# Gate's and the first units' products of a third's first block ahead of the second block's tiles, in the input projection of a hybrid trunk layer

## The chip, the cores and the metric

The kernel runs on one core of one Trainium2 chip. The core has five engines with a queue each: TensorE (PE; its weight loads are shown apart as PEld), VectorE (DVE), ScalarE (ACT), GpSimd (POOL) and SyncE (SP), which here issues nearly all DMA transfers. An engine works through its queue in order, and semaphores tie the engines together. The metric is the device time of one execution in microseconds (us), as a median over runs.

## The reference

One layer of a trunk with three parallel head groups (DEPTH is 1), on 2048 tokens with 16 meta tokens ahead, 1024 wide, all in float32:

```
h = concatenate([meta, x])                          # 2064 tokens x 1024
p = rms_norm(h, norm_mix_pre) @ w_in                # one combined input projection
oa = rg_lru_group(p's first 512 columns)            # gated linear recurrence
ob = forgetting_attention_group(q, k, v, f_logit)   # softmax attention, 8 heads, decay from f_logit
oc = rwkv7_group(the remaining columns)             # matrix-state recurrence over the tokens
h = h + rms_norm(concatenate([oa, ob, oc]) @ w_out, norm_mix_post)
f = causal_dwconv(rms_norm(h, norm_ffn_pre) @ ffn_up)
h = h + rms_norm((gelu(gate) * val) @ ffn_down, norm_ffn_post)
return h[16:]
```

The change concerns the second line alone: the norm of the tokens, and their products with `w_in`. `f_logit` are 8 of its columns (2048 to 2055); the kernel calls their product gate.

## The kernel before

**Stages.** First the input projection (until about 850 us of the profile), with the two recurrences running beside it, then attention with the rest of the recurrences, the output projection, and the feed-forward layer.

**Precision.** A float32 product is made of three: each operand is split into a high part, rounded for TensorE's fast format, and a low part, the remainder, and `mm3` (lines 185 to 189) adds high x high, high x low and low x high in PSUM. So a weight of the projection is a pair `wh`, `wl`, and the tokens are a pair `xh`, `xl`.

**Thirds, blocks, tiles.** The tokens are taken in three thirds (`part` 0, 1, 2), so that the recurrences can begin on a third while the next is projected. `w_in_tokens` cuts 17 tiles (the meta tokens, and 16 of 128) into two blocks for each third: 400 and 384 tokens, 384 and 384, 256 and 256. A tile is brought in by `norm_transpose` (line 133): a load of 128 x 1024 into the ring `nt_x` of four buffers (line 137, SP), the sum of squares (line 124, ACT), the root (lines 127 and 128, DVE and POOL), the scaling (line 142, DVE), eight transposes (line 155, PE), and for each half of the tile the copy `xh` (line 161, ACT) and the remainder `xl` (line 162, DVE). ACT's sum of squares is kept behind the last rounding of weights (`core.rounded`) for the tiles of the second third beyond its first two.

**Gate and units.** `w_in_part` is a generator that runs over a third. `w_in_gate` loads gate's weights `fw` (made in the first third, kept in DRAM, loaded again at line 318), and its `products` takes 16 products on a block (lines 323 and 324), whose two parts ACT and DVE add (lines 326 and 328). Then come 24 units of 128 columns: 8 for RWKV-7, 4 for the RG-LRU, 4 each for k, v and q. A unit's pair of weights is loaded by `w_in_weights` (in the later thirds two transfers of 512 KB from DRAM, line 250), and `w_in_step` makes 24 products on a block (lines 187 to 189), copies the result out of PSUM and stores it. The pairs live in a ring of two (`w`); in the last third every other two units use the ring `nt_x` instead. Before, gate's weights in the later thirds also take one buffer of the ring of pairs, the `wh` side.

**The first third is done otherwise.** Its second block's tiles are held back in `core.unturned`, gate and the first two units are run on the first block, with `core.turn_tile` bringing in one tile after each step, and only then gate and those two units on the second block. In the later thirds, all tiles of both blocks come first, then gate on both blocks, and then the units, each on both blocks. The last two units of every third, both of q, are run together block by block.

**The passages.** A passage is the end of one third and the start of the next. The main loop (lines 2247 to 2304) calls `w_in_norm` for the next third behind the last unit of a third. At each `yield` of `w_in_part` the loop moves the recurrences on by 1.25 steps on average (`Beside`), and at whole units in the later thirds it also issues a step of `w_out_split` and of `up_sums`, whose loads (line 1786, POOL operations at 1788 and 1790) are kept behind the last weight load on SP (`core.loaded`). The recurrences' work on PE near the passages has lines 1159, 1190, 1213, 1218, 1450; on DVE 1171 to 1188 and 1443.

**What sets the order.** The text gives priorities, not the final order. The program is built with

```python
    with _tile.TileContext(nc, schedule_with_timeline_sim=True) as tc:
```

so a planner orders each engine's queue by a modelled time: among the instructions that it takes to be ready, the one earlier in the text goes first. `issue_after` adds an order by hand. The queue is then fixed, and on the chip an instruction that isn't ready holds up all behind it.

Of the kernel before, what the change touches and what calls it, by code (L numbers as in the profile page):

```python
# [194 lines left out]
def w_in_tokens(part):  # L195

    tiles = [(0, META)] + [(META + P * i, P) for i in range(SEQ // P)]
    cuts = ((0, 4, 7), (7, 10, 13), (13, 15, 17))[part]
    return [tiles[a:e] for a, e in zip(cuts, cuts[1:])]


def w_in_norm(core, pools, psum, x, meta, gain, part):
    blocks = []
    for b, tl in enumerate(w_in_tokens(part)):
        t0 = tl[0][0]
        n = sum(r for _, r in tl)
        hi = pools["xn"].tile([P, KD, n], F32R, tag=f"xh{b}", name=core.n("xh"))
        lo = pools["xn"].tile([P, KD, n], F32R, tag=f"xl{b}", name=core.n("xl"))
        blocks.append((t0, n, tl, hi, lo))

    def tile(block, s, rows):
        t0, _, _, hi, lo = block
        src = meta if s < META else x[s - META : s - META + rows, :]
        late = part == 1 and (s, rows) not in blocks[0][2][:2]
        after = (lambda: core.tc.issue_after(core.rounded.ins)) if late else nullcontext
        norm_transpose(core, pools, psum, src, rows, gain, [(hi, lo, s - t0, 0, rows)], after)

    core.unturned = []
    for block in blocks:
        for s, rows in block[2]:  # L220
            if part == 0 and block is blocks[1]:
                core.unturned.append((block, s, rows))
            else:
                tile(block, s, rows)
    core.turn_tile = lambda: tile(*core.unturned.pop(0))
    return blocks


def w_in_kept(scr, c0):

    return scr["wk"][c0 // P]


def w_in_weights(core, pools, w_in, c0, scr, part, raw=None):

    src = w_in[:, c0 : c0 + P].rearrange("(k p) c -> p k c", p=P)
    if raw is not None:
        pair = hi, lo = [pools["w"].tile([P, KD, P], F32R, tag=s, name=core.n(s)) for s in ("wh", "wl")]
        core.loaded = core.nc.sync.dma_start(raw, src)
        core.rounded = core.nc.scalar.activation(hi[:], raw, AF.Copy)  # L240
        core.nc.vector.tensor_tensor(lo[:], raw, hi[:], op=ALU.subtract)
    elif part == 0:
        pair = split_load(core, pools["w"], (pools["nt"], "nt_x", None), src, [P, KD, P], "w")
    else:
        core.turns += part == 2
        pl, tags = (pools["nt"], ("nt_x", "nt_x")) if core.turns % 4 > 1 else (pools["w"], ("wh", "wl"))
        pair = [pl.tile([P, KD, P], F32R, tag=tag, name=core.n(s)) for s, tag in zip(("wh", "wl"), tags)]
    for t, kept in zip(pair, w_in_kept(scr, c0)):
        t = t[:].rearrange("p k c -> p (k c)").bitcast(F32)
        core.loaded = core.nc.sync.dma_start(*((kept, t) if part == 0 else (t, kept)))  # L250
    return pair
# [51 lines left out]
def w_in_gate(core, pools, psum, w_in, blocks, scr, part):  # L303

    nc = core.nc
    c0 = 2048
    home, tag = ("w", "wh") if part else ("us", "us")
    w = pools[home].tile([P, KD, P], F32R, tag=tag, name=core.n("fw"))
    flat, kept = w[:].rearrange("p k c -> p (k c)").bitcast(F32), w_in_kept(scr, 3 * D)[0]
    if part == 0:  # L310
        raw = pools["st"].tile([P, KD, 8], F32, tag="stv", name=core.n("fraw"))
        nc.sync.dma_start(raw[:], w_in[:, c0 : c0 + 8].rearrange("(k p) c -> p k c", p=P))
        nc.vector.memset(w[:].bitcast(F32), 0.0)
        nc.scalar.activation(w[:, :, 0:8], raw[:], AF.Copy)
        nc.vector.tensor_tensor(w[:, :, 32:40], raw[:], w[:, :, 0:8], op=ALU.subtract)
        nc.sync.dma_start(kept, flat)
    else:
        nc.sync.dma_start(flat, kept)

    def products(t0, n, tl, hi, lo):  # L320
        ps = psum.tile([P, 512], F32, tag="mm", name=core.n("psf"))
        for k in range(KD):
            nc.tensor.matmul(ps[:, :n], w[:, k], hi[:, k], start=k == 0, stop=False)
            nc.tensor.matmul(ps[:, :n], w[:, k], lo[:, k], start=False, stop=k == KD - 1)
        a = pools["st"].tile([8, 400], F32, tag="sth", name=core.n("fa"))
        nc.scalar.activation(a[:, :n], ps[32:40, :n], AF.Copy)
        o = pools["st"].tile([8, 400], F32, tag="stl", name=core.n("fo"))
        nc.vector.tensor_tensor(o[:, :n], ps[0:8, :n], a[:, :n], op=ALU.add)
        nc.sync.dma_start(scr["f"][:, t0 : t0 + n], o[:, :n])

    return products


def w_in_part(core, pools, psum, w_in, blocks, scr, part):
    gate = w_in_gate(core, pools, psum, w_in, blocks, scr, part)
    units = [("c", 2056 + P * i) for i in range(8)] + [("a", P * i) for i in range(4)]
    units += [(s, c + P * i) for s, c in (("k", 1024), ("v", 1536), ("q", 512)) for i in range(4)]
    waiting = [None]

    def step(*args):  # L340

        after = w_in_step(core, pools, psum, *args, scr)
        if waiting[0]:
            waiting[0]()
        waiting[0] = after

    if part == 0:
        raws = pools["rp"].tile([P, 2, KD, P], F32, tag="rw_e", name=core.n("raw"))
        firsts = [
            (w_in_weights(core, pools, w_in, c0, scr, part, raws[:, i]), kind, c0)  # L350
            for i, (kind, c0) in enumerate(units[:2])
        ]
        for i, block in enumerate(blocks):
            gate(*block)
            yield i > 0
            for w, kind, c0 in firsts:
                step(w, block, kind, c0)
                if i == 0:
                    core.turn_tile()
                yield i > 0  # L360
            while core.unturned:
                core.turn_tile()
        del units[:2]
    else:
        for block in blocks:
            gate(*block)
        yield False
        yield True

    for kind, c0 in units[:-2]:  # L370
        w = w_in_weights(core, pools, w_in, c0, scr, part)
        for block in blocks:
            step(w, block, kind, c0)
            yield block is blocks[-1]

    last = [(w_in_weights(core, pools, w_in, c0, scr, part), kind, c0) for kind, c0 in units[-2:]]
    for block in blocks:
        for w, kind, c0 in last:
            step(w, block, kind, c0)
            yield kind == "q" and c0 == last[-1][2]  # L380
# [2123 lines left out]
```

## Time and profile before

| | |
|---|---|
| median of 3 runs | 2953.49 us (2950.68 to 2956.22) |
| the profiled execution | 2962.62 us |
| its span, first to last instruction | 2960.9 us |
| mean granted TensorE clock | 0.976 |
| instructions | 53225 |

All rows of the trace are from the one profiled execution; their times count from the start of its span. A row of the timeline has start, length, engine, line, operation, `out<-in` by the program's names, shapes and count, and in brackets the idle time ahead with what ended it. Matmuls overlap, so the length of one (0.34 us) is longer than the distance from one start to the next. The input projection's thirds end near 267 and 597 us.

### The profile page before, as it was taken

The numbers are of one execution on the slowest core, as the hardware profiler recorded it, in microseconds if no ns is written. First come the engines' busy times: TensorE is split into PE (matmuls) and PEld (weight loads), VectorE is DVE, ScalarE is ACT, GpSimd is POOL, SyncE is SP. The second block draws the span as 40 slices with busy tenths as digits, with TensorE's granted clock in tenths as the row PEclk, the third lists the DMA queues.
The fourth block names the chain that finished last, engine by engine and source line by source line (L and its number), as shares of the span: only waits on it lengthen the run. The fifth ranks groups of instructions, "written<-read, shape, count | busy, mean of one in ns | idle before, by whom it ended". The sixth has DMA issues, their size and how long they took to land.

```text
span 2960.9 us, 53225 instructions
## 1 busy us (share of the span) xinstructions
PE 2844.5 (96%) x18854; PEld 2448.4 (83%) x18854; DVE 2002.2 (68%) x3839; ACT 1505.8 (51%) x2937; POOL 1297.3 (44%) x1572
## 2 busy tenths in 40 slices
PE   7998999999978889999999999999999999999998
PEld 7997989989865555566578999999999999787887
DVE  4257654666578765556656998888777787646766
ACT  4236442554346655555635666666566665324333
POOL 1002221222114667666723667355655544656443
PEclk9999999999988999999999999999999999999999
DMA  6776678577653357435255665577777774436453
GB/s 218 248 245 203 198 249 290 166 245 234 203 126 73 87 127 222 108 102 139 58 158 173 209 188 174 164 234 207 215 202 224 218 197 141 146 116 218 149 171 121
DMA packets 470343, 530.51 MB, mean 179 GB/s; under 512 B 86862, under 2 KB 356888, under 8 KB 468524
## 3 DMA queue, kind: packets, MB, share of 16 engines
q1 hardware_dynamic: 469308, 526.18, 58.9%
q8 instruction: 148, 2.42, 0.3%
q0 software_dynamic: 768, 0.93, 0.1%
q14 instruction: 119, 0.97, 0.1%
HBM read 368.07 MB, written 158.90 MB: 178 GB/s over the span
## 4 chain that ended last, share of the span: by engine, by line
PE 69%; DVE 7%; ACT 6%; DMA 5%; issue 2%; POOL 2%; SPq 1%; DVEq 0%; ACTq 0%; POOLq 0%
PE psu L187 9%; PE psu L188 9%; PE psu L189 9%; PE po L779 4%; PE psd L187 4%; PE psd L188 4%; PE psd L189 4%; PE psp L187 2%; PE psp L189 2%; PE psp L188 2%; PE sc L756 2%; PE mx L627 2%; PE sc L757 2%; PE pswo L187 2%; PE pswo L188 2%
## 5 line engine op out<-in xcount | busy, mean ns | idle before, releaser
L188 PE MATMUL psu<-xo,uw 128*128 128x344 f32 x1848 | 591.5, 320 | 0.0
L187 PE MATMUL psu<-xo,uw 128*128 128x344 f32 x1848 | 585.8, 322 | 3.3 <-ACT u L1933 2.3
L189 PE MATMUL psu<-xo,uw 128*128 128x344 f32 x1848 | 582.0, 320 | 0.3 <-DVE uw L1762 0.2
L187 PE MATMUL psp<-xh,wh 128*128 128x384 f32 (+2 forms) x1152 | 383.0, 333 | 0.4 <-DVE rww L1462 0.3
L188 PE MATMUL psp<-xl,wh 128*128 128x384 f32 (+2 forms) x1152 | 378.3, 328 | 0.0
L189 PE MATMUL psp<-xh,wl 128*128 128x384 f32 (+2 forms) x1152 | 375.6, 326 | 0.0
L1762 DVE TENSOR_TENSOR uw<-uq,uw 128x512 fp32r<-128x512 f32 x341 | 319.0, 940 | 60.6 <-ACT uw L1761 57.5
L187 PEld LDWEIGHTS psu<-xo,uw 128*128 128x128 f32 x1848 | 345.8, 188 | 4.8 <-ACT u L1933 2.6
L188 PEld LDWEIGHTS psu<-xo,uw 128*128 128x128 f32 x1848 | 347.1, 188 | 0.0
L189 PEld LDWEIGHTS psu<-xo,uw 128*128 128x128 f32 x1848 | 345.7, 188 | 1.2 <-DVE uw L1762 1.1
L1761 ACT ACTIVATE uw<-uq 128x512 fp32r<-128x512 f32 x462 | 288.1, 627 | 98.1 <-PE psu L189 41.1
L761 ACT ACTIVATE p<-sc,bias 128x512 f32<-128x512 f32 (+4 forms) x352 | 196.8, 590 | 164.3 <-PE sc L757 134.9
L632 DVE TENSOR_REDUCE mc<-mx 128x1 f32<-128x512 f32 (+5 forms) x352 | 191.8, 565 | 113.6 <-PE mx L627 83.7
L1901 DVE SCALAR_TENSOR_TENSOR uy<-psu,ffn_cols,uy 128x342 f32<-128x342 f32 (+1 forms) x390 | 220.5, 567 | 61.1 <-ACT uy L1899 59.7
L1909 POOL TENSOR_TENSOR uy<-uy,uy 128x342 f32<-128x342 f32 (+1 forms) x132 | 145.8, 1105 | 230.6 <-DVE uy L1901 58.4
L1762 POOL TENSOR_TENSOR uw<-uq,uw 128x512 fp32r<-128x512 f32 x121 | 183.3, 1515 | 133.7 <-ACT uw L1761 111.5
L187 PEld LDWEIGHTS psp<-xh,wh 128*128 128x128 f32 x1152 | 220.4, 191 | 7.7 <-issue 4.4
L188 PEld LDWEIGHTS psp<-xl,wh 128*128 128x128 f32 x1152 | 220.5, 191 | 5.6 <-issue 3.9
L189 PEld LDWEIGHTS psp<-xh,wl 128*128 128x128 f32 x1152 | 220.3, 191 | 4.3 <-issue 3.0
L800 POOL TENSOR_TENSOR acc<-acc,p 128x512 f32<-128x512 f32 (+3 forms) x186 | 196.4, 1059 | 49.8 <-DVE acc L800 22.2
L1762 DVE TENSOR_TENSOR fo<-u,fo 128x896 fp32r<-128x896 f32 x88 | 102.0, 1159 | 130.0 <-ACT fo L1761 129.4
L1761 ACT ACTIVATE fo<-u 128x896 fp32r<-128x896 f32 x88 | 81.2, 923 | 205.9 <-PE psd L189 118.3
(492 smaller groups left out, 6289.8 us busy)
## 6 DMA issues: line engine op xcount, KB each, us to landing
uq<-scr_us SPq DMA_DIRECT2D x220, 256.0 KB
uq<-in_ffn_up_dram SPq DMA_DIRECT2D x209, 256.0 KB
wl<-scr_wk SPq DMA_DIRECT2D x48, 512.0 KB
wh<-scr_wk SPq DMA_DIRECT2D x48, 512.0 KB
u<-scr_ff SPq DMA_DIRECT2D x88, 256.0 KB
scr_ff<-uy SPq DMA_DIRECT2D x110, 171.0 KB
raw<-in_w_in_dram SPq DMA_DIRECT2D x24, 512.0 KB
scr_wk<-wh SPq DMA_DIRECT2D x24, 512.0 KB
```

Of the source, the lines that this page charges most:

```text
L187: nc.tensor.matmul(out, ah, bh, start=first, stop=False, skip_group_check=more)
L188: nc.tensor.matmul(out, ah, bl, start=False, stop=False, skip_group_check=more)
L189: nc.tensor.matmul(out, al, bh, start=False, stop=last, skip_group_check=more)
L627: nc.tensor.matmul(ps[:rows, : e - a], q3[:, qo : qo + rows], k2[:, a:e], start=True, stop=not last)
L632: self.reduced = nc.vector.tensor_reduce(mc[:rows, i, ci : ci + 1], ps[:rows, : e - a], axis=AX.X, op=ALU.max)
L761: last = nc.scalar.activation(p[:rows, :w], ps[:rows, :w], AF.Exp, bias=bias[:rows, j : j + 1])
L779: mm = nc.tensor.matmul(po[at : at + 64, c0:n], v1[:rows, j], p[:rows, : n - c0], start=start and i < 2, stop=end and i + 2 >= len(group), ...
L800: eng.tensor_tensor(a, ps_[0][0][:rows, c0:n] if start and i == 1 else a, p[:rows, : n - c0], op=ALU.add)
L1761: core.nc.scalar.activation(hi, src, AF.Copy)
L1762: (eng or core.nc.vector).tensor_tensor(lo, src, hi, op=ALU.subtract)
L1901: core.conved = stt(y[:, :n], src[:, i : n + i], cw[:, 44 * i + cc : 44 * i + cc + 1], y[:, :n], op0=ALU.mult, op1=ALU.add)
L1909: core.pooled = nc.gpsimd.tensor_tensor(v[:, :n], g[:, :n], v[:, :n], op=ALU.mult)
```

## The change

Three edits.

- `w_in_norm` holds back the second block's tiles in every third, not the first alone.
- `w_in_gate` takes its weights in the second third from the ring of tiles (`nt_x`, four buffers) instead of the ring of pairs. In the last third they stay with the pairs.
- `w_in_part` drops the other branch: in every third gate and the first units run on the first block, a tile of the second block is brought in after each of these steps, the rest of the tiles after them, and then gate and the same units run on the second block. The first units are two in the first and second third, one in the last. Their weights are asked for behind gate's weights and ahead of its products. In the first third they still pass through the buffer `raws`. The count of yields in a third stays the same.

```diff
@@ -218,7 +218,7 @@
     core.unturned = []
     for block in blocks:
         for s, rows in block[2]:
-            if part == 0 and block is blocks[1]:
+            if block is blocks[1]:
                 core.unturned.append((block, s, rows))
             else:
                 tile(block, s, rows)
@@ -304,7 +304,7 @@
 
     nc = core.nc
     c0 = 2048
-    home, tag = ("w", "wh") if part else ("us", "us")
+    home, tag = (("us", "us"), ("nt", "nt_x"), ("w", "wh"))[part]
     w = pools[home].tile([P, KD, P], F32R, tag=tag, name=core.n("fw"))
@@ -346,26 +346,21 @@
 
     if part == 0:
         raws = pools["rp"].tile([P, 2, KD, P], F32, tag="rw_e", name=core.n("raw"))
-        firsts = [
-            (w_in_weights(core, pools, w_in, c0, scr, part, raws[:, i]), kind, c0)
-            for i, (kind, c0) in enumerate(units[:2])
-        ]
-        for i, block in enumerate(blocks):
-            gate(*block)
+    firsts = [
+        (w_in_weights(core, pools, w_in, c0, scr, part, *((raws[:, i],) if part == 0 else ())), kind, c0)
+        for i, (kind, c0) in enumerate(units[: 2 if part < 2 else 1])
+    ]
+    for i, block in enumerate(blocks):
+        gate(*block)
+        yield i > 0
+        for w, kind, c0 in firsts:
+            step(w, block, kind, c0)
+            if core.unturned:
+                core.turn_tile()
             yield i > 0
-            for w, kind, c0 in firsts:
-                step(w, block, kind, c0)
-                if i == 0:
-                    core.turn_tile()
-                yield i > 0
-            while core.unturned:
-                core.turn_tile()
-        del units[:2]
-    else:
-        for block in blocks:
-            gate(*block)
-        yield False
-        yield True
+        while core.unturned:
+            core.turn_tile()
+    del units[: len(firsts)]
 
     for kind, c0 in units[:-2]:
         w = w_in_weights(core, pools, w_in, c0, scr, part)
```

## The prediction

> **What bounds the kernel now.** I read the busy shares first, then the windows of the input projection, then the queues of TensorE (PE), VectorE (DVE) and SyncE (SP) in the two passages.
>
> ```profile
> PE 2844.5 (96%) x18854; PEld 2448.4 (83%) x18854; DVE 2002.2 (68%) x3839; ACT 1505.8 (51%) x2937; POOL 1297.3 (44%) x1572
> 310.00:590.00 280.00, 276.96 (x2615) 252.33 (x2614) 167.40 (x404) 117.25 (x226) 63.66 (x95) 0.99 0.72 234
> 630.00:900.00 270.00, 243.94 (x2789) 217.47 (x2790) 179.40 (x498) 126.88 (x273) 57.28 (x101) 0.93 0.64 188
> ```
>
> A windows row gives start:end, length, then the busy time of PE, PEld, DVE, ACT and POOL, the granted clock, the DMA share and GB/s. PE is busy 96% of the span. Between the passages (310 to 590) it is busy 276.96 of 280 us: time saved ahead of this stretch on PE moves the whole stretch forward. After the second passage 26 us of 270 are idle, so there a part of a saving could be lost to other waits.
>
> The passage from the first to the second third, split where PE's state changes:
>
> ```profile
> 267.00:270.00 3.00, 2.74 (x24) 2.49 (x23) 2.79 (x10) 2.01 (x4) 0.00 (x0) 1.00 0.89 218
> ...
> 272.30:278.70 6.40, 0.00 (x0) 0.00 (x0) 6.40 (x12) 2.20 (x5) 3.30 (x4) 0.69 1.07 378
> 278.70:282.00 3.30, 3.29 (x14) 2.07 (x14) 2.17 (x5) 1.83 (x3) 1.09 (x2) 0.50 1.01 400
> ...
> 286.00:289.30 3.30, 3.30 (x19) 3.06 (x17) 3.30 (x8) 2.72 (x6) 0.00 (x0) 0.65 0.16 36
> 267.00:300.00 33.00, 26.20 (x153) 20.59 (x152) 26.47 (x52) 17.24 (x36) 5.94 (x6) 0.79 0.58 191
> ```
>
> PE is idle 33.00 - 26.20 = 6.8 us here, nearly all of it in one hole from 272.3 to 278.7. DVE is busy through the whole hole (6.40 of 6.40). Behind the hole the granted clock is 0.50. What that costs is read from equal work at both clocks:
>
> ```profile
> 267.11 0.34 PE L189 MATMUL psp<-xh,wl 128*128 128x384 f32 x1
> 267.29 1.80 PE L155 MATMUL pst<-ident,xt 128*128 128x128 f32 x15
> 269.35 0.63 PE L1159 MATMUL eps<-ident,rwe 128*128 128x128 f32 x4 [0.26 <-DVE rwe L82]
> 269.81 2.36 PE L155 MATMUL pst<-ident,xt 128*128 128x128 f32 x17
> 278.71 0.79 PE L1213 MATMUL rps<-rwrav,rwbk 64*128 64x128 f32 x2 [6.54 <-DVE rwbk L1181]
> ...
> 280.06 0.79 PE L1213 MATMUL rps<-rwrav,rwbk 64*128 64x128 f32 x2
> 284.08 2.07 PE L1190 MATMUL eps<-rwsq,bones 128*128 128x512 f32 x2
> 285.94 3.08 PE L155 MATMUL pst<-ident,xt 128*128 128x128 f32 x16
> 288.78 0.42 PE L323 MATMUL psf<-xh,fw 128*128 128x384 f32 x1
> 290.53 0.48 PE L1213 MATMUL rps<-rwrav,rwbk 64*128 64x128 f32 x2
> 291.31 0.48 PE L1213 MATMUL rps<-rwrav,rwbk 64*128 64x128 f32 x2
> 592.51 1.02 PE L1190 MATMUL eps<-rwsq,bones 128*128 128x512 f32 x2
> ```
>
> A pair of L1213 and L1218 groups takes 280.06 - 278.71 = 1.35 us slow and 291.31 - 290.53 = 0.78 us fast; four slow pairs lose 2.3 us. L1190 takes 285.94 - 284.08 = 1.86 us against 1.02, so 0.8 lost. The 16 transposes take 288.78 - 285.94 = 2.84 us against 16/15 x 1.80 = 1.9, so 0.9 lost. The slow clock costs 4.0 us, and **the passage loses 6.8 + 4.0 = 10.8 us**.
>
> The second passage, from the third's end at 596.9:
>
> ```profile
> 596.90:598.60 1.70, 1.64 (x14) 1.36 (x12) 1.56 (x8) 1.53 (x5) 0.00 (x0) 1.00 1.00 397
> 598.60:600.50 1.90, 0.00 (x0) 0.03 (x1) 1.70 (x8) 0.85 (x2) 0.00 (x0) 1.00 0.86 294
> 600.50:603.60 3.10, 3.10 (x25) 2.81 (x25) 3.10 (x7) 2.45 (x5) 0.00 (x0) 1.00 0.83 214
> 603.60:607.65 4.05, 3.80 (x28) 3.37 (x28) 4.05 (x9) 1.99 (x5) 3.07 (x4) 1.00 0.85 301
> ```
>
> Here the hole is 1.9 us, the clock stays at 1.00, and 0.25 us follow: some **2.2 us** in all.
>
> **The change, part by part.** It adds no product, transpose or transfer. It moves them; the sum is a matter of which waits remain.
>
> *Why the hole lasts until 278.7.* The instruction that ends it is a recurrence product behind DVE's L1181. DVE's queue there:
>
> ```profile
> 269.59 1.88 DVE L162 TENSOR_TENSOR xl<-pst,xh 128x512 fp32r<-128x512 f32 x3
> 272.84 1.28 DVE L162 TENSOR_TENSOR xl<-pst,xh 128x512 fp32r<-128x512 f32 x2
> 275.84 1.88 DVE L162 TENSOR_TENSOR xl<-pst,xh 128x512 fp32r<-128x512 f32 x3
> 277.64 1.02 DVE L1181 SCALAR_TENSOR_TENSOR rwbk<-rwe 128x512 f32<-128x512 f32 x1
> 282.58 1.28 DVE L142 SCALAR_TENSOR_TENSOR xt<-xt,rs,g_pre 128x1024 f32<-128x1024 f32 x1
> ```
>
> Each tile needs two L162, so these eight are four tiles; the recurrence's own operations stand between them. Before, gate's products come after all six tiles. The last two tiles' loads were issued at 274.36 and ACT met the first at 280.04:
>
> ```profile
> 266.10 0.41 SPq L318 DMA_DIRECT2D fw<-scr_wk  x1
> 271.06 0.34 SPq L250 DMA_DIRECT2D wh<-scr_wk  x1
> 274.36 1.28 SPq L137 DMA_DIRECT2D xt<-in_x_dram  x2
> 300.27 0.35 SPq L250 DMA_DIRECT2D wh<-scr_wk  x1
> 280.04 1.06 ACT L124 ACTIVATE xj<-xt 128x1024 bf16<-128x1024 f32 x1 [3.78 <-DMA xt<-in_x_dram]
> ```
>
> *After.* Only three tiles come first: 24 transposes at 1.80 / 15 = 0.12 us, with L1159 and its wait between, end near 271. Gate's first half (k 0 to 3) needs the third tile's first L162, the fifth in the queue; if DVE keeps its order, it ends at 274.1. The second half needs the sixth, at 276.5. So PE idles 3.1 us, runs eight products, idles 1.0 us more, and goes on. L1181 is no longer behind the fourth tile's two L162 (2 x 0.62), so L1213 is ready at 277.4, about when gate ends (277.9). Idle left: 0.3 + 3.1 + 1.0 = 4.4 us instead of 6.8.
>
> *Cover for the second block.* Gate's ring slot makes three late tiles instead of two. From 277.9 PE has the work behind gate: two units of 24 products on 384 columns, one each 0.18 us (267.11 to 267.29, start to start), 8.6 us, the L1213 pairs (four, 3.1 us) and L1190 (1.0 us), together 12.7 us, to about 290. The late loads wait for slots that the first transposes free at about 268.5 to 271; at before's 5.7 us from issue to use, even issues at 274 to 276 give data by 282, and each tile then costs 1.06 us on ACT and 1.28 + 2 x 0.62 on DVE: three are through by about 290. That is just enough. Were this cover gone, a missing tile would cost 2 to 3 us; I take 1 us (ends 0 and 3).
>
> *Weights.* Gate's weights go to the tiles' ring and no longer wait for the pair that unit q frees, so they are there early. The first unit's and second unit's pairs can then be asked for when the last two units end; before, the second's had to wait for gate, till 300.27. That is 1 MB more ahead of 283 and 0.5 MB of gate less. Moved at the 378 GB/s of the window 272.3 to 278.7 the added 0.5 to 1 MB is 1.3 to 2.7 us of transfer, in front of the same late tiles; it is inside the 0 to 3 us above. On SP the unit sums' loads follow the last weight load, so they come later; POOL, which works on them, is busy 44% of the span.
>
> *Clock.* With the gap cut to 3.1 us the clock may or may not fall. The nearest row is the hole of 2.15 us at 631.85, in a stretch with a mean clock of 0.91:
>
> ```profile
> 631.85 0.75 PE L1298 MATMUL rps<-rwxu,rwsc 32*32 32x32 f32 x64 [2.15 <-ACT rwsc L1251]
> 620.00:640.00 20.00, 17.85 (x274) 16.97 (x273) 10.29 (x32) 13.05 (x29) 8.00 (x16) 0.91 0.72 226
> ```
>
> A mean of 0.91 over 20 us is 1.8 us of clock lost; the 1.9 us hole of the second passage lost none. Ends 0 and 4.0, taken 0.9, half of 1.8.
>
> [...]
>
> *Second passage.* Gate keeps its place among the pairs. PE's stop at 598.6 is for DVE's L1443, a recurrence operation that the change doesn't touch:
>
> ```profile
> 600.50 0.41 PE L1450 MATMUL rps<-ident,rww 128*128 128x128 f32 x2 [1.97 <-DVE rww L1443]
> 600.68 0.41 SPq L250 DMA_DIRECT2D wh<-scr_wk  x1
> 600.74 1.88 DVE L162 TENSOR_TENSOR xl<-pst,xh 128x512 fp32r<-128x512 f32 x3
> 607.65 0.36 PE L187 MATMUL psp<-xh,wh 128*128 128x256 f32 x1 [0.25 <-DVE rww L1462]
> ```
>
> The first block's L162 start only at 600.74, and the first unit's wh is issued at 600.68, so gate's and that unit's products can't fill the hole ahead. Moved forward they may even meet their weights too early. I take 0.5 us of gain, ends -2 and +2.2.
>
> **The sum.** First passage after: 4.4 idle + 0.9 clock + 1.0 new waits = 6.3 us, against 10.8: 4.5 gained. With 0.5 of the second passage, 5.0 us. The profiled execution took 2962.6 us (span 2960.9); it would take 2957.6. The median of the three runs, 2953.5, is 9.1 below it, and I carry the same difference over: **2948.5 us**. A measurement here can tell about 0.2%, 5.9 us, from no change, and the forecast lies just inside that.
>
> **Rivals.**
>
> *The hole closes wholly* (2942). With gate's products in front, DVE's copies of the first block may be placed ahead of the recurrence's operations; then gate starts at about 272, the clock never falls, and 10.8 plus some of the second passage go, say 11.5 us. For it: from 269.59 to 276.5 six L162 take 3.7 us (0.62 each), so 3.2 us of recurrence work stands between them. Against it: that recurrence work was there first in the queue, and the change says nothing about it.
>
> *It is hidden or given back* (2953). The recurrence's chain through DVE may set the pace: DVE is busy 26.47 of 33 us, and PE's freed time could return as waits behind the recurrence or for the late tiles, and after 630, where 26 us idle are spread, as waits for transfers. For it: the hole's releaser is the recurrence, not a tile. Against it: 276.96 of 280 us busy in between.
>
> *Slower* (2959.5). The second block's norm (L142) is placed in DVE's queue ahead of the first block's last L162 and L1181, while its load lands late. DVE is in order, so gate's second half and the recurrence wait behind it. Place: 272 to 286. It decides from the point where the fourth tile lands later than DVE comes to it, about 276; before, its like landed at 280. Then L142 ends at 283.9 as now, one L162 and L1181 follow, and PE stands from 271 to about 285.5 but for 1.4 us of gate: 13.1 idle and the 4.0 of clock, 17 against 10.8, so 6 us more.
>
> **How the numbers follow.** Forecast (gain 2 to 8) 0.44, closed wholly 0.22, given back 0.19, slower 0.15. Of the forecast's share a little under half lies beyond 5.9 us: faster 0.20 + 0.22 = 0.42. The rest of it and the third case make same 0.24 + 0.18 = 0.42; slower 0.16. The range runs from the wholly closed hole with the second passage's 2.2 us and some luck in the new order (2938) to the slower rival (2960).
>
> **What would show it.** Right: after the last transposes of the first block a gap of about 3 us and then L323 and L324 ahead of L155; wh and wl of two units issued before 280; the clock at or near 1.00 from 278 to 289; the first unit's products of the first block before 285. Wrong: L1213 still ending a gap of over 5 us; PE standing on L155 or on L323 of the second block around 285 to 292; a row in the second passage where L187 waits for wh; or new idle between 310 and 900 that takes the gain back.

## The result, and the profile after

| | before | after |
|---|---|---|
| median | 2956.21 us | 2964.80 us |
| ratio, 95% interval | | 1.0029 [1.0016, 1.0043] |
| profiled execution's span | 2960.9 us | 2960.8 us |

After is slower by some 8.6 us, where 2948.5 us was forecast, with a range to 2960. One execution each of after (3436 us), of n4 below (3262) and of before (3549, in a later session) ran at a clock under 0.8, and the ratios leave them out. That the two spans are equal is chance: the other executions of before on record lie between 2945.3 and 2966.5 us, and the profiled one of before lay high (2962.6) and that of after low (2962.5). A second profile of before, taken later (e0 below), has a span of 2955.8.

The page of after, its line of busy time:

```profile
PE 2837.4 (96%) x18854; PEld 2444.0 (83%) x18854; DVE 1994.5 (67%) x3839; ACT 1505.0 (51%) x2937; POOL 1300.4 (44%) x1572
```

**First passage.** The windows of after (start:end, length, busy time of PE, PEld, DVE, ACT, POOL, clock, DMA share, GB/s), the first being the one in which PE was idle for 6.8 us before:

```profile
267.00:300.00 33.00, 28.47 (x167) 24.16 (x166) 26.83 (x51) 17.44 (x35) 7.38 (x7) 0.90 0.59 198
300.00:310.00 10.00, 7.13 (x99) 6.15 (x98) 6.14 (x19) 9.75 (x23) 1.65 (x6) 0.77 0.25 85
```

PE's idle time in the first window fell from 6.8 to 4.5 us, as the change meant it to, and the clock rose from 0.79 to 0.90. But in the ten microseconds behind it PE is now idle for 2.9 us, against 0.5 before (its row is below). The waits of PE between 255 and 330 us (engine, line, releaser: sum, times, longest):

```profile
PE psf L323 <- ACT xh L161: 3.9, 2, 2.7
PE psf L324 <- DVE xl L162: 2.6, 1, 2.6
PE eps L1154 <- DVE rwe L82: 0.7, 1, 0.7
```

Before, one wait of 6.5 us (L1213 for DVE's L1181) stood here. The timeline of after tells where each of the new ones comes from (L1154 is before's L1159; lines behind 370 moved up by five):

```profile
270.57 1.49 SPq L137 DMA_DIRECT2D xt<-in_x_dram  x2
...
272.29 0.45 PE L323 MATMUL psf<-xh,fw 128*128 128x384 f32 x1 [1.28 <-ACT xh L161]
275.60 0.69 PE L324 MATMUL psf<-xl,fw 128*128 128x384 f32 x1 [2.56 <-DVE xl L162]
...
285.49 1.74 DVE L142 SCALAR_TENSOR_TENSOR xt<-xt,rs,g_pre 128x1024 f32<-128x1024 f32 x1
290.25 0.49 PE L155 MATMUL pst<-ident,xt 128*128 128x128 f32 x3
...
300.11 1.80 PE L155 MATMUL pst<-ident,xt 128*128 128x128 f32 x15
302.25 0.60 ACT L161 ACTIVATE xh<-pst 128x512 fp32r<-128x512 f32 x1
302.87 1.28 ACT L1565 ACT_TABLE_LOAD   x1
304.48 1.55 ACT L161 ACTIVATE xh<-pst 128x512 fp32r<-128x512 f32 x3
305.60 0.69 PE L323 MATMUL psf<-xh,fw 128*128 128x384 f32 x1 [2.66 <-ACT xh L161]
```

The first block's share sums to what was forecast: 0.69 + 1.28 + 2.56 = 4.5 us. The second block's tiles were scaled (L142) by 287.2, but most of their transposes (L155) came only at 300.1, because the text has them behind the first units' steps; the copies (L161) came behind recurrence work and a table load (1.28 us) on ACT, and gate's first product on the second block waited 2.66 us for them. And the clock:

```profile
274.60:281.40 6.80, 5.80 (x18) 5.80 (x19) 4.78 (x11) 2.69 (x6) 1.22 (x2) 0.50 1.06 369
305.30:312.10 6.80, 6.29 (x79) 5.72 (x80) 5.49 (x16) 5.29 (x14) 1.86 (x4) 0.50 0.14 41
```

And two windows of before:

```profile
275.00:288.70 13.70, 9.99 (x41) 6.63 (x42) 11.62 (x21) 6.24 (x13) 5.94 (x6) 0.51 0.67 253
300.00:310.00 10.00, 9.54 (x117) 8.87 (x115) 6.00 (x22) 9.76 (x22) 3.56 (x9) 1.00 0.31 104
```

Two stretches of 6.8 us at half clock, where before had one of 13.7 us: in this profile one hole became several, with no less idle time and no less slow clock. PE is busy for 5.80 and 6.29 us of the two. Products on 384 columns start 0.32 us apart there (276.08 to 276.40) against 0.17 us just behind (281.50 to 281.67), so nearly half of that is lost: 6.0 us by an estimate that counts it as half. Counted in the same way, before lost half of 9.99, 5.0 us.

**Second passage.** The waits of PE from 590 to 700 us, and the timeline around the first:

```profile
PE psp L187 <- DMA wh<-scr_wk: 3.6, 1, 3.6
PE rps L1445 <- DVE rww L1438: 3.1, 2, 1.7
```

```profile
599.57 2.18 SPq L1781 DMA_DIRECT2D us<-in_ffn_up_dram  x4
601.52 0.41 PE L1445 MATMUL rps<-ident,rww 128*128 128x128 f32 x2 [1.69 <-DVE rww L1438]
601.85 0.41 SPq L250 DMA_DIRECT2D wh<-scr_wk  x1
...
603.69 0.39 PE L324 MATMUL psf<-xl,fw 128*128 128x256 f32 x1 [0.62 <-DVE xl L162]
...
608.48 0.39 PE L187 MATMUL psp<-xh,wh 128*128 128x256 f32 x1 [3.57 <-DMA wh<-scr_wk]
```

The old hole (L1445, before's L1450) is still there, 1.69 us. The first unit's products, now at the front of the third, then wait 3.57 us for `wh`: SP issued it at 601.85, behind four loads of the unit sums, and PE starts 6.6 us later. Before, PE had all the tiles' transposes, gate's products on the first block and recurrence work to do until 607.65.

### The profile page after: what moved, and what is told of

Its sections match the earlier page's. It is cut to its first block, busy times and chain, and to the rows that moved or that the text cites. A ratio compares the mean times of both kernels' runs of the same rounds, so it can differ in the third digit from the quotient of the medians.

```text
span 2960.8 us, 53229 instructions
## 1 busy us (share of the span) xinstructions
PE 2837.4 (96%) x18854; PEld 2444.0 (83%) x18854; DVE 1994.5 (67%) x3839; ACT 1505.0 (51%) x2937; POOL 1300.4 (44%) x1572
## 4 chain that ended last, share of the span: by engine, by line
PE 66%; DMA 8%; DVE 7%; ACT 4%; POOL 3%; issue 2%; SPq 1%; DVEq 0%; POOLq 0%; ACTq 0%
PE psu L187 9%; PE psu L188 9%; PE psu L189 9%; PE psd L187 4%; PE psd L188 4%; PE psd L189 4%; PE po L774 4%; PE psp L188 2%; PE psp L189 2%; PE psp L187 2%; PE pswo L187 2%; PE pswo L189 2%; PE pswo L188 2%; PE sc L751 2%; PE mx L622 2%
## 5 line engine op out<-in xcount | busy, mean ns | idle before, releaser
L187 PE MATMUL psu<-xo,uw 128*128 128x344 f32 x1848 | 586.2, 322 | 2.6 <-DVE vb L1948 1.9
L189 PE MATMUL psu<-xo,uw 128*128 128x344 f32 x1848 | 582.0, 320 | 0.4 <-DVE uw L1757 0.3
L187 PE MATMUL psp<-xh,wh 128*128 128x384 f32 (+2 forms) x1152 | 380.7, 331 | 3.6 <-DMA wh<-scr_wk 3.6
L189 PE MATMUL psp<-xh,wl 128*128 128x384 f32 (+2 forms) x1152 | 375.6, 327 | 0.6 <-DMA wl<-scr_wk 0.6
L187 PEld LDWEIGHTS psu<-xo,uw 128*128 128x128 f32 x1848 | 345.9, 188 | 4.3 <-DVE vb L1948 3.0
L189 PEld LDWEIGHTS psu<-xo,uw 128*128 128x128 f32 x1848 | 345.7, 188 | 1.1 <-DVE uw L1757 1.1
L187 PEld LDWEIGHTS psp<-xh,wh 128*128 128x128 f32 x1152 | 219.6, 191 | 9.7 <-DMA wh<-scr_wk 3.8
L189 PEld LDWEIGHTS psp<-xh,wl 128*128 128x128 f32 x1152 | 219.7, 191 | 5.5 <-issue 3.3
L795 POOL TENSOR_TENSOR acc<-acc,p 128x512 f32<-128x512 f32 (+3 forms) x186 | 196.4, 1059 | 46.6 <-DVE acc L795 21.3
```

Source lines behind the costliest of these rows:

```text
L187: nc.tensor.matmul(out, ah, bh, start=first, stop=False, skip_group_check=more)
L189: nc.tensor.matmul(out, al, bh, start=False, stop=last, skip_group_check=more)
L795: eng.tensor_tensor(a, ps_[0][0][:rows, c0:n] if start and i == 1 else a, p[:rows, : n - c0], op=ALU.add)
```

## The experiments

Each kernel was timed against before in the same session. "Stretch" is the time from the last product of the second third to the end of the fifth unit of the last third (the 768th and the 848th L189 row), which holds the second passage. The times of both columns are those of each kernel's one profile. Baselines of 2955.5 to 2958.6 us were measured for before.

| label | edit | median us | ratio, 95% interval | second third us | stretch us |
|---|---|---|---|---|---|
| (before) | | 2956.21 | | 329.6 | 70.2 |
| (after) | | 2964.80 | 1.0029 [1.0016, 1.0043] | 331.3 | 75.7 |
| e0 | before again | 2957.02 | 0.9997 [0.9985, 1.0008] | 329.3 | 69.1 |
| e1 | first passage alone | 2953.44 | 0.9990 [0.9980, 0.9999] | 328.5 | 72.6 |
| e2 | second passage alone | 2979.22 | 1.0078 [1.0065, 1.0091] | 330.0 | 75.7 |
| e4 | after, unit sums' loads later | 2974.83 | 1.0058 [1.0044, 1.0071] | 330.1 | 81.9 |
| e3 | after, gate's weights of the last third in the tiles' ring | 2964.97 | 1.0026 [1.0012, 1.0039] | 329.9 | 72.2 |
| e3b | the same, second passage alone | 2954.72 | 0.9988 [0.9976, 1.0000] | 328.9 | 68.7 |
| n4 | before + 12 memsets | 2971.43 | 1.0040 [1.0025, 1.0055] | 329.4 | 71.9 |
| n24 | before + 24 memsets | 2957.71 | 0.9999 [0.9988, 1.0011] | 328.6 | 69.3 |
| n5 | before + 40 memsets | 2964.60 | 1.0026 [1.0016, 1.0036] | 330.2 | 70.5 |
| n70 | before + 70 memsets | 2963.73 | 1.0028 [1.0014, 1.0041] | 329.6 | 70.8 |
| a24 | after + 24 memsets | 2963.93 | 1.0021 [1.0007, 1.0036] | 330.5 | 77.3 |
| b0 | before + barrier | 2993.87 | 1.0124 [1.0108, 1.0140] | 328.5 | 69.2 |
| b1 | after + barrier | 2999.19 | 1.0147 [1.0125, 1.0169] | 328.9 | 77.8 |
| b2 | first passage alone + barrier | 2998.07 | 1.0141 [1.0123, 1.0159] | 330.3 | 70.0 |
| b3 | second passage alone + barrier | 3000.85 | 1.0147 [1.0129, 1.0166] | 331.2 | 76.3 |

**Which passage loses?** The control, and each passage alone. In e1 and e2 the new branch of `w_in_part` and the held-back tiles are taken only in some thirds; e2 keeps gate's old home in the second third (set against after, cut where "..." stands):

```diff
-            if block is blocks[1]:
+            if part in (0, 1) and block is blocks[1]:      # e1;  (0, 2) in e2
...
+    if part in (0, 1):                                     # e1;  (0, 2) in e2
         firsts = [
...
+    else:
+        for block in blocks:
+            gate(*block)
+        yield False
+        yield True
```

> The kernel before, once more, as a control. Every theory: a ratio of 1.000 within 0.0015, no verdict. Its profile is a second look at the attention stage, where the first profile of before lost 7 us against after (the landmark 200 score groups in came 0.3 us later in after, while the projection's end came 7.0 us later): if that was one execution's bad luck, this profile's span is some 5 to 8 us shorter than 2960.9 and its projection still ends near 856.

> Only the first passage is changed (gate's weights have the homes that the change gives them; the second passage is as before). Theory: the first passage gives back what it gains, because one hole of 6.5 us and 13.7 us of half clock became three holes of together 7 us and two half-clock stretches of together 13.7 us. So the second third ends 1 to 2 us later than before (598 against 596.7), nothing follows from it, and the time is +1 us, ratio 1.000 to 1.001. Rival A (the loss comes from the first passage): the whole +8 us, ratio 1.003. Rival B (any new order of the units costs in the last third, whichever passage is changed): +3 to +6 us, ratio 1.001 to 1.002.

> Only the second passage is changed (first passage and its gate weights as before). Theory: the first unit's products in front of the second block's tiles wait for their wh, which SP issues behind four loads for the unit sums; the hole of 3.57 us and 1.7 us of lost clock behind it, less the 2 us that the old holes cost, and then the shifted last third: +5 to +7 us, ratio 1.0017 to 1.0025, and the row L187 waiting for wh at about 607. Rival A (the loss comes from the first passage): +0 to 1 us, ratio 1.000. Rival B (any new order costs): +3 to +6 us, the same as the other half alone.

The control gave 0.9997. Its span is 5.1 us shorter than that of the first profile, as expected for a profile without bad luck, but the projection, which was expected to end near 856 as before, ended at 850.8: the difference arose there and not in the attention stage. The first passage alone gave no loss (0.9990), so rivals A and B are out. The second alone cost 20 us and more, far above what was expected of it. Windows of e0 and of e2: the stretch, then from the projection's end to the last row of the tile `mx` in the attention stage:

```profile
593.33:662.40 69.07, 63.24 (x767) 58.02 (x767) 47.02 (x125) 37.73 (x80) 19.94 (x35) 0.98 0.72 237
850.56:1500.16 649.60, 595.34 (x3725) 369.79 (x3724) 429.72 (x1022) 352.67 (x699) 395.07 (x570) 0.94 0.47 116
```

```profile
595.23:670.97 75.74, 68.08 (x778) 61.31 (x777) 45.71 (x125) 38.44 (x82) 19.71 (x35) 0.91 0.69 222
858.67:1521.98 663.31, 601.42 (x3659) 367.01 (x3658) 426.78 (x1014) 353.30 (x697) 395.78 (x570) 0.94 0.46 114
```

The stretch is 6.7 us longer, as in after. But e2 loses another 13.7 us where the change edits nothing, in the attention stage. There its queues hold the work in another order than before's: the planner, which works by modelled times, sorted the later stages anew. That became a theory of its own (theory P below).

**Is it the loads of the unit sums ahead of wh?** e4 puts that step one unit later:

```diff
-                    if part and i % 2 == 0:
+                    if part and i > 1 and i % 2 == part - 1:
```

> After, with the step that brings in the unit sums of the last third (1 MB of loads on SP) put one unit later, so that wh and wl of the first unit and of the next pair are issued ahead of it. Theory: L187 no longer waits 3.57 us for wh, the clock behind it stays at 1.00, and 4 to 6 us come back: +2 to +4 us against before, ratio 1.0007 to 1.0014. Rival A (first passage): still +8 us, 1.003. Rival C (the wait for wh is only the first of several that the shifted last third has, such as the unit sums' own loads, now later): the wait at 607 goes and comes back after 620, still +7 to +10 us.

Rival C is nearest, but the wait didn't go, and the loss of some 16 us is above its 7 to 10. Waits of PE in e4, 590 to 700 us:

```profile
PE rps L1348 <- ACT rww L1339: 4.2, 1, 4.2
PE psp L187 <- DMA wh<-scr_wk: 3.1, 1, 3.1
```

The wait for `wh` stays at 3.1 us although no load of the unit sums stands ahead of it on SP. The pair takes the place of the last q unit's pair in the ring, which is given back only when that unit ends, at 595.4. SP issued `wh` at 596.35, and PE started on it 6.4 us later, at 602.71. So from this place in the ring the first unit's weights can't be early, whatever is ahead of them. The edit isn't clean, though: the planner also put this unit's first product ahead of most of gate's (PE came to it at 599.6, in after at 604.9), so how much the loads alone cost in after isn't shown. And a wait of 4.2 us followed behind, with the stretch at 81.9 us.

**Can the weights be had earlier?** With gate's weights in the tiles' ring, the first unit's pair gets the place of the last but one unit:

```diff
-    home, tag = (("us", "us"), ("nt", "nt_x"), ("w", "wh"))[part]
+    home, tag = (("us", "us"), ("nt", "nt_x"), ("nt", "nt_x"))[part]
```

> After, with gate's weights in the last third in the tiles' ring too, so that the first unit's pair takes the ring place that the last but one unit of q frees (about 5 us earlier than the place it had). Theory W (the second passage loses because the first unit's wh comes too late): no row of L187 waiting for wh at 602 to 609, from the second third's end to the third unit of the last third 39 to 43 us as before (after took 47), so 4 to 6 us less than after by the end of the projection. For the whole time, what the later stages' new order gives or takes (theory P: up to 10 us either way) comes on top. Rival V (it loses because any work in front leaves the late tiles standing in DVE's and ACT's queues): the wait for wh goes, but PE stands on L323 and L324 of the second block instead, and the stretch stays at 46 to 48 us.

> The same in the second passage alone, the first passage as before. Theory W: the stretch of the second passage again 39 to 43 us, projection's end within 3 us of before's. Rival V: 46 to 48 us. Since the first passage gave no gain above 2 us, the two kernels should not differ in the projection by more than that; what they differ beyond it belongs to the later stages' order (theory P).

The row of L187 waiting for `wh` is gone in both, and the stretch is 72.2 and 68.7 us, that of the kernels without the change. But the expectation named the time to the end of the third unit, and there e3 took 46.6 us, as rival V has it, and e3b 43.2, at the upper end of theory W; after has 47.0, and the two profiles of before 43.1 and 39.1. And the projection ends no earlier: from the second third's end it takes 267.6 us in e3 and 265.4 in after. Waits of PE in e3 (590 to 700), and of DVE (660 to 674):

```profile
PE rps L1389 <- DVE rstate L1393: 4.4, 1, 4.4
PE rps L1293 <- POOL us L1785: 1.8, 1, 1.8
PE pst L155 <- DVE xt L142: 1.6, 1, 1.6
```

```profile
DVE rwxu L1281 <- DMA rwxu<-dx: 7.2, 1, 7.2
```

A new wait stands behind the stretch: DVE is held 7.2 us at L1281 by a small transfer of the recurrence (8 KB each), and PE's L1389, whose operand is copied by the instructions queued behind that on DVE, waits 4.4 us. e3b has the same 4.4 us. Rival V's row (PE on the late tiles, L155) exists too, with 1.6 us in e3 and 0.7 in e3b. In e3 6.8 us at half clock follow it.

A fair mark is one where the kernels have done the same work. At the end of the fifth unit those with the changed second passage have run 10 matmul instructions more than before, at the third 32 more; at the end of the seventh, 950 are behind the second third's end in all. Windows up to there, of before, after and e3b:

```profile
596.71:683.38 86.67, 79.81 (x952) 72.89 (x952) 57.27 (x152) 41.36 (x89) 23.87 (x39) 0.98 0.73 241
598.07:690.41 92.34, 81.78 (x951) 74.17 (x951) 57.94 (x155) 39.98 (x85) 23.09 (x39) 0.96 0.68 215
593.17:685.10 91.93, 82.71 (x952) 74.86 (x951) 58.41 (x157) 40.95 (x87) 25.79 (x40) 0.94 0.70 222
```

e3 has 95.4 us. So early weights remove the wait for `wh`, and with it what it cost up to the fifth unit, but by the seventh as much is lost again, to other waits (9.2 us of idle time in e3b, against 6.9 in before) and to the clock (0.94 against 0.98).

**What is a new order worth?** n4, n5, n24 and n70 are before with small memsets (0.07 us each) that nothing reads. In the text they stand behind the projection; the planner puts them into gaps of DVE's first 14 (n4) to 43 us (n70):

```diff
+        for _ in range(12):          # 24, 40, 70
+            nc.vector.memset(nul[:], 0.0)
         beside.finish()
```

In n4's trace 1,912 of TensorE's 18,854 matmul instructions then stand at another place than in before's, all behind the projection; in n24's none. In n5 and n70 it is 1,284 and 1,378, from 775 us on, where the last third's units are still running.

> The kernel before with 12 small DVE memsets (0.06 us each) in the text behind the input projection. They change nothing of the projection, but the planner puts PE's, DVE's and ACT's work of the attention stage in another order behind them. Theory P (the planner's new order of the later stages moves the time by itself, which is how the second passage alone came to cost 20 us where its projection lost only about 7): the projection's marks as in before (third ends 264 and 593, projection's end 850 to 856), and between 850 and 1500 a change of at least 4 us up or down, ratio off 1.000 by 0.0015 or more. Rival Q (the order of the later stages is worth nothing, what was lost there came from the projection's late or early end): ratio 1.000 within 0.0012.

> The same with 40 memsets (2.4 us of DVE in all), which give a third order of that stage. Theory P: again off 1.000 by 0.0015 or more, by another amount than the 12 memsets, perhaps of the other sign. Rival Q: 2.4 us on DVE at most, ratio 1.000 to 1.001.

> The kernel before with 24 of the small DVE memsets (0.07 us each, which the planner puts into gaps of DVE's first 20 us). With this number TensorE's order of the whole kernel comes out as in before. Theory P (new orders of the later stages were what cost 16 us and 9 us with 12 and 40 memsets): ratio 1.000 within 0.0012. Rival M (the memsets themselves cost, at the start of DVE's queue): between the other two, 1.002 to 1.004.

> Before with 70 memsets, again another order behind the projection. Theory P: some time between 1.000 and 1.005 that cannot be told from here; with 0, 12, 24 and 40 it shows the spread that orders have. Rival M: more than with 40, over 1.004.

12 memsets cost 0.40%, 24 cost nothing (0.9999), 40 and 70 cost 0.26% and 0.28%. Rival M is out with n24, rival Q with the other three. Windows of n4 and of n24 from the projection's end to the last `mx` row (e0: 649.60):

```profile
852.09:1512.70 660.61, 601.54 (x3726) 372.55 (x3724) 435.13 (x1022) 352.00 (x699) 397.01 (x570) 0.94 0.47 114
```

```profile
857.10:1504.60 647.50, 591.16 (x3725) 367.80 (x3724) 426.00 (x1022) 352.49 (x699) 396.05 (x570) 0.95 0.47 117
```

The number of rows is practically the same, and n4 takes 11.0 us more than e0: 660.61 - 601.54 = 59.1 us idle against 54.3, and 6.2 us more of busy time for the same products. A single profile doesn't divide this safely: n24, with the order of e0, has 56.3 us idle and 4.2 us less of busy time than e0, at a clock of 0.95 against 0.94. The ratios carry the point: an order alone, with not one product moved in the projection (n4), is worth as much as the whole effect under study, and the three new orders of before were all worse than its own.

> After with 24 memsets: both passages in after's order, some 230 of TensorE's 14113 rows in another order near 900 to 1050 us. Theory S with P: the stretch from the second third's end to the fifth unit of the last third stays at 75 to 78 us (before: 69 to 73), and the whole time differs from after's 1.0029 by some 0.001 to 0.003, either way. Rival T (passages neutral): it can come out at 1.000 with the stretch at 70.

a24 kept both passages, and the stretch (77.3); its 1.0021 is not far enough from after's 1.0029 to tell the two apart.

**The change without the new order.** With a barrier of all engines behind the projection, TensorE's order in b1's trace is the same as in b0's from 1017 us of b1 on (1005 of b0), some 155 us behind the projection's last product; up to there the two still differ. In b3 it differs again from 1683 us of b0 on. The edit:

```diff
+        tc.strict_bb_all_engine_barrier()
         beside.finish()
```

> The kernel before, with a barrier of all engines in the text between the input projection and what is left of the recurrences. It costs something of its own (10 to 40 us, since the attention stage can no longer begin beside the projection's end), and it is the base for the next three: behind it the planner's order of the later stages is nearly the same in this kernel and in the next two.

> After with the same barrier; TensorE's order is the same as in the kernel before with the barrier from early in the attention stage on. What this takes more than that one is what the change costs by itself. Theory S (the second passage's waits cost 5 us, the first passage gives back what it gains, the rest of what has been seen is the later stages' order): +3 to +7 us. Rival T (the passages are neutral, all of it is the later order): -1 to +2 us. Rival U (the passages cost the whole +8.6): +8 to +11 us.

> Only the first passage changed, with the barrier. Theory S: -1 to +2 us against before with the barrier. Rival: if the -3 us that this edit gave without a barrier was its own, -2 to -4 us.

> Only the second passage changed, with the barrier (the order behind it is the same up to the output projection, and differs from there). Theory S: +3 to +7 us up to the end of the attention stage, not the 20 us that this edit cost without a barrier. Rival: still +15 us or more, then the second passage does cost that by itself.

Against b0 the medians differ by +5.3 (b1), +4.2 (b2) and +7.0 us (b3). In ratios b1 is 0.0023 above b0, with an interval of about 0.0027 either way: in the middle of theory S, but the rivals are not excluded by it. What is clear is b3: the second passage alone, which cost 20 us and more without the barrier, costs 7 with it, give or take about 7. b2 came out higher than theory S has it, though its second third and its stretch are those of before within the scatter. In its profile the loss is behind the projection: the stretch to the last `mx` row takes 698.8 us at a clock of 0.90, in b0's 688.9 at 0.92, with nearly the same idle time (76.2 and 77.5 us). These are the slowest of b2's four executions and the fastest of b0's.

**All of them together.** The stretch, as windows of one kernel without the changed second passage (n70) and one with it (b1):

```profile
599.59:670.44 70.85, 61.79 (x768) 56.52 (x767) 45.81 (x126) 37.84 (x80) 19.59 (x35) 1.00 0.70 230
```

```profile
592.79:670.57 77.78, 68.26 (x777) 61.87 (x777) 45.65 (x125) 38.28 (x82) 19.79 (x35) 0.91 0.67 219
```

Nine profiles with the old second passage (both of before, e1, the four with memsets, b0, b2) have 69.1 to 72.6 us, 70.4 in the mean. Five with after's (after, e2, a24, b1, b3) have 75.7 to 77.8, 76.6 in the mean. The two don't overlap: the changed second passage costs 6.2 us in its place. To the end of the seventh unit the nine have 85.5 to 89.1 us, 86.8 in the mean, and the five 92.1 to 94.3, 92.9 in the mean: 6.0 us. From the windows of the stretch in all fourteen, idle time is 9.6 against 6.4 us in the mean, and the clock 0.926 against 0.967 (an estimate of what that loses, the stretch times what its clock lacks of 1: about 5.7 against 2.3 us). For the first passage, seven profiles that have it changed take 328.5 to 331.3 us for the second third, 330.0 in the mean, and ten that don't take 328.5 to 331.2, 329.5 in the mean: it is worth nothing, in either direction, within 1 us. The clock behaves differently in the two groups. All ten old ones have one stretch of 13.7 us at half clock that goes with the hole, in before from about 275 on, inside it (n4 and b3 another of 3.4). The seven changed ones have two stretches each, of 6.8 us in after, e4 and b2, but of 3.4 us in e1, e3, a24 and b1. Those of e1:

```profile
271.60:275.00 3.40, 3.15 (x10) 3.15 (x11) 2.97 (x7) 0.89 (x1) 0.00 (x0) 0.50 1.06 402
302.30:305.70 3.40, 2.98 (x70) 2.92 (x71) 2.09 (x7) 3.29 (x9) 0.62 (x2) 0.50 0.13 43
```

So in four of seven the slow clock was halved, and yet their second thirds, 329.5 us in the mean, are no shorter than the old ones.

## Why the prediction was wrong

**First passage, idle time: right in sum for the first block, wrong behind it.** "Idle left: 0.3 + 3.1 + 1.0 = 4.4 us instead of 6.8": measured 4.5. The cause is the one forecast, DVE's L162 for the third tile, but the terms aren't: the fifth L162 ended at 275.5 instead of 274.1, the wait for it was split by two products that needed only ACT's copies (1.28 + 2.56), and the 1.0 us for the sixth didn't come. So the agreement to 0.1 us is partly luck. The step that failed is the cover for the second block: "That is just enough ... I take 1 us (ends 0 and 3)". The data were in time (the tiles were scaled by 287, against "through by about 290"), and PE's other work lasted longer than forecast; what was late were their transposes, which the new text puts behind the unit steps, and then ACT, whose queue held recurrence work and a table load ahead of the copies. The price was 2.9 us, the upper end.

**First passage, clock: wrong.** "Ends 0 and 4.0, taken 0.9". The forecast priced one fall of the clock, behind the longest hole, at even odds. The clock fell twice in all seven profiles with this passage changed; in after for 6.8 us each, as long in all as the 13.7 us of before, at an estimated cost of 6.0 us. In after's trace the holes of 1.28 and 2.56 us, 0.75 us of work apart, came with 6.8 us at half clock (from 274.60), and so did the hole of 2.66 us (from 305.30).

By this count after loses 4.5 + 2.9 + 6.0 = 13.4 us here, not 6.3. The forecast's 10.8 for before took the clock at 4.0, from equal work at both clocks; counted as after is, with the ten microseconds behind, before loses 6.8 + 0.5 + 5.0 = 12.3. The gain of 4.5 us was none: the second third took 1.7 us longer in after's profile, and 0.5 us longer in the mean of all.

**Second passage: the sign was seen, and not priced.** "Moved forward they may even meet their weights too early. I take 0.5 us of gain, ends -2 and +2.2." It lost 6.2 us. The prediction's rows would have allowed a price: the first unit's `wh` was issued at 600.68 in before, and a tile of the first passage took 5.7 us from issue to use, so products at the front of the third would stand until about 606. The experiments on this point: with the weights early (e3, e3b) the stretch is back at 72.2 and 68.7 us, but by the seventh unit the loss is there again; with the loads ahead of them gone (e4) PE still waits 3.1 us. So the wait for `wh` is shown as the first cause of the loss, not as the only one. The row that the prediction named as its refutation, L187 waiting for `wh`, is the longest wait of the passage.

**The later stages: a term that was missing.** "Time saved ahead of this stretch on PE moves the whole stretch forward" took the rest of the kernel as fixed. It isn't: the planner orders it by modelled times, and any edit that shifts these gives another order. The same edit of the first passage moves the ratio by -0.0010 from before (e1), by -0.0049 from e2 to after, and by +0.0038 from e3b to e3. These don't add, though the first passage itself is worth nothing in the profiles. Carried over as a term, it would have been 0 to +12 us by the ratios of the meaningless edits (n24, n4), more than twice the gain of 5.0 us that the prediction added up.

**The rivals.** In the first passage the given-back rival came: what PE gained in front returned as a wait for the late tiles (2.66 us), and the second third was no shorter. Its 2953 left the second passage and the later order out. The hole didn't close wholly. The slower rival's mechanism (the second block's L142 ahead of L1181 on DVE) didn't occur; its 2959.5 was nearest by accident.

**What stays open** is how after's 8.6 us divide. The second passage's 6.2 are shown where they arise; whether they reach the end in full, and what the new order adds or gives back, isn't settled (b1 against b0: +5.3, with an interval wider than that). After's profile ends the projection at 863.5 us, the two of before at 856.5 and 850.6; from there to the last `mx` row it takes 644.1 us, they 651.2 and 649.6. But after has 3660 matmul instructions in that stretch and before 3725, so part of both differences is recurrence work that was moved ahead. Nor is it shown what holds the kernels with early weights back (e3 stays at 1.0026, e3b comes to 0.9988); the wait of DVE for the recurrence's transfer is the row that stands there. No version here beats before by more than the measurement can tell: e1 and e3b are at 0.9990 and 0.9988, with intervals that reach 0.9999 and 1.0000.

## What to carry to other kernels

Work that is pulled forward into a gap must have its operands there, so price it from the point where its buffer is freed, not from where its load stands in the queue (here, in e4, the buffer was free at 595.4, and PE used the weights at 602.71 although no load of the unit sums stood ahead of theirs). Where a planner orders the queues from modelled times, first measure what a meaningless edit does to the time (here 0 to +12 us by the ratios): an effect smaller than that is not seen in the total and must be measured in its own stretch, over several profiles. And a gap that is split in two may cost as much clock as the whole one did (here in three profiles of seven, two stretches of 6.8 us at half clock against one of 13.7).

## What the runs showed of the hardware

The half clock came in the passages in lengths of 3.4 (e1), 6.8 (after), 10.2 (e2) and 13.7 us (before), and whether it came after a hole of 1.96 to 1.97 us, and for how long, did not follow from the hole's length in the three runs below. PE stands for 1.2 to 2.0 us at the start of the last third in fifteen of the seventeen profiles, ahead of the same instruction, released by the same DVE line. The prediction's row of before has 1.97 us there, and the window behind it (before):

```profile
598.60:602.00 3.40, 1.50 (x12) 1.43 (x13) 3.20 (x11) 1.70 (x4) 0.00 (x0) 1.00 0.85 265
```

The same in e1 (the line is L1451 there), timeline and window:

```profile
595.80 0.63 PE L1451 MATMUL rps<-ident,rww 128*128 128x128 f32 x2 [1.96 <-DVE rww L1444]
```

```profile
595.80:599.20 3.40, 3.40 (x14) 3.11 (x15) 3.05 (x6) 1.54 (x3) 0.00 (x0) 0.51 0.91 251
```

And in e2:

```profile
599.25 0.41 PE L1451 MATMUL rps<-ident,rww 128*128 128x128 f32 x2 [1.97 <-DVE rww L1444]
```

```profile
600.30:610.50 10.20, 8.31 (x35) 7.09 (x34) 4.26 (x9) 1.80 (x5) 2.90 (x4) 0.50 0.87 308
```

The hole of 1.96 to 1.97 us cost no clock in before, was followed by 3.4 us at half in e1, and by 10.2 us at half in e2, where a second wait followed. So a hole of 2 us cost from 2 us to at most some 6 us here, by an estimate from these rows (1.97, and half of the 8.31 us that PE was busy in the 10.2), and one execution doesn't tell which.
